# A rotation kernel: the buffers of the last eight outputs, taken in the other order

## Chip, cores, metric

The kernel runs on one core of one Trainium2 chip. The metric is device time in microseconds (us), lower is better. The runs were made on several chips, and the kernel before was timed again each time: its median was 1269.72, 1269.82, 1270.10 and 1269.99 us, and a single run of it 1269.89 us.

## The reference

```python
x = np.random.randn(8192, 8192).astype(np.float32)
np.rot90(x, 1)          # counter-clockwise: out[i, j] = x[j, 8191 - i]
```

It is a pure move: 268.44 MB are read and 268.44 MB written, and nothing is computed.

## The kernel before

The matrix is cut into 16 macro tiles of 1024 rows by 4096 columns, the last of them into two of 512 rows. A macro tile is loaded in pieces of 128 rows (2 MB each, issued on the SP queue). DVE copies each load, with the columns reversed in groups of 128, into eight small tiles `ar`, and after that the load buffer is free. PE transposes 128x128 blocks of `ar` into PSUM, ACT copies 2048 columns of PSUM at a time into an output buffer, and stores the output (2 MB, issued on the ACT queue). There are two load buffers (`a_pool`) and two output buffers (`o_pool`), 16 KB per partition each.

```python
    a_pool = ctx.enter_context(tc.tile_pool(name="a_pool", bufs=2))
    r_pool = ctx.enter_context(tc.tile_pool(name="r_pool", bufs=68))
    o_pool = ctx.enter_context(tc.tile_pool(name="o_pool", bufs=2))
    # ... cut ...
    def store(r0, rt, c0, chunks, end, first):
        # ... cut: rows = rt * P; PW and G, column blocks per PSUM tile and per output ...
        for i, g0 in enumerate(range(0, W // P, G)):
            if end and (i + first) % 2 == 0:
                ot = a_pool.tile([P, F], dt, tag="a")
            else:
                ot = o_pool.tile([P, F], dt, tag="o")
            # ... cut: S ...
            for h in range(0, G, PW):
                # ... cut: 16 transposes on PE into the PSUM tile ps ...
                nc.scalar.copy(o[:, G - PW - h : G - h, :], ps)
                done = h + PW
                if done % S == 0:
                    # ... cut: dst ...
                    nc.scalar.dma_start(out=dst, in_=o[:, G - done : G - done + S, :])

    *most, before_last, last = tiles
    for m in most:
        store(*m, load(*m), False, 0)

    c1 = load(*before_last)
    c2 = load(*last)
    store(*before_last, c1, True, 1)
    store(*last, c2, True, 1)
```

The two last macro tiles have four outputs each, here called O1 to O8. When they are made no further load is to come, so that the load buffers serve as output buffers too. With `first` 1 the order is o, a, o, a and again o, a, o, a. The output made just before O1, the last of the macro tile before, is called o8 below, and the one before that o7.

Of the kernel before, what the change touches and what calls it, by code (L numbers as in the profile page):

```python
# [2 lines left out]

# [5 lines left out]

P = 128  # L10




R = 1024
RT = R // P
LAST = [4, 4]
W = 4096
CH = 512
F = 4096  # L20
FP = 2048


def whole_reads(nc):






    for fn in nc.m.functions:
        for block in fn.blocks:
            for n, ins in enumerate(block.instructions):
                if not isinstance(ins, mybir.InstDMACopy):
                    continue
                src = ins.ins[0]
                ap = [list(d) for d in src.ap]
                if len(ap) == 3 and ap[2][0] == 1 and ap[1][0] == ap[2][1]:
                    ap = [ap[0], [1, 1], [1, ap[1][1] * ap[2][1]]]
                    block.instructions[n] = copy.replace(  # L40
                        ins,
                        ins=[copy.replace(src, ap=ap)],
                        ant_dge_precooked=False,
                    )


def macro_tiles(N, M):

    tiles = [(r0, RT, c0) for r0 in range(0, N, R) for c0 in range(0, M, W)]
    r0, _, c0 = tiles.pop()  # L50
    for n in LAST:
        tiles.append((r0, n, c0))
        r0 += n * P
    return tiles


@with_exitstack
def kernel(
    ctx: ExitStack,
    tc: tile.TileContext,  # L60
    x: bass.AP,
    k: bass.AP,
    out: bass.AP,
):
    nc = tc.nc
    assert k == 1, f"only k=1 supported, got {k}"
    nc.at_finalize(whole_reads)

    N, M = x.shape
    dt = x.dtype  # L70

    consts = ctx.enter_context(tc.tile_pool(name="consts", bufs=1))
    ident = consts.tile([P, P], dt)
    make_identity(nc, ident)
# [4 lines that stand above are left out]
    psum_pool = ctx.enter_context(  # L79
        tc.tile_pool(name="psum", bufs=2, space=bass.MemoryType.PSUM)  # L80
    )

    loads = 0

    def load(r0, rt, c0):





        nonlocal loads
        chunks = {}
        for t in range(rt):


            if loads < RT and loads % 4 >= 2:
                a = o_pool.tile([P, W], dt, tag="o")
            else:
                a = a_pool.tile([P, W], dt, tag="a")
            loads += 1  # L100
            nc.sync.dma_start(  # L101
                out=a[:], in_=x[r0 + t * P : r0 + (t + 1) * P, c0 : c0 + W]
            )
            for j in range(W // CH):
                ar = r_pool.tile([P, CH // P, P], dt, tag="ar")
                nc.vector.tensor_copy(  # L106
                    out=ar[:],
                    in_=a[:, j * CH : (j + 1) * CH].rearrange(
                        "r (b m) -> r b m", m=P
                    )[:, :, ::-1],  # L110
                )
                chunks[t, j] = ar
        return chunks

    def store(r0, rt, c0, chunks, end, first):





        rows = rt * P
        PW = 1
        while 2 * PW * rows <= FP:
            PW *= 2
        G = PW
        while 2 * G * rows <= F:
            G *= 2
        for i, g0 in enumerate(range(0, W // P, G)):
            if end and (i + first) % 2 == 0:
                ot = a_pool.tile([P, F], dt, tag="a")  # L130
            else:
                ot = o_pool.tile([P, F], dt, tag="o")
            o = ot[:, : G * rows].rearrange("m (g f) -> m g f", g=G)

            S = PW if end and r0 + rows == N and g0 + G == W // P else G
            for h in range(0, G, PW):
                pt = psum_pool.tile([P, FP], mybir.dt.float32, tag="ps")
                ps = pt[:, : PW * rows].rearrange("m (g f) -> m g f", g=PW)
                for w in range(PW):
                    g = g0 + h + w  # L140
                    for t in range(rt):
                        nc.tensor.transpose(  # L142
                            ps[:, PW - 1 - w, t * P : (t + 1) * P],
                            chunks[t, g * P // CH][:, g % (CH // P), :],
                            ident,
# [5 lines that stand above are left out]
                    top = M - c0 - (g0 + done) * P  # L151
                    dst = out[top : top + S * P, r0 : r0 + rows].rearrange(
                        "(g m) f -> m g f", g=S
                    )
                    nc.scalar.dma_start(  # L155
                        out=dst, in_=o[:, G - done : G - done + S, :]
                    )

    tiles = macro_tiles(N, M)
    *most, before_last, last = tiles  # L160
    for m in most:
        store(*m, load(*m), False, 0)

    c1 = load(*before_last)
    c2 = load(*last)
    store(*before_last, c1, True, 1)
    store(*last, c2, True, 1)


# [1 line left out]
_INS = ['x', 'k']  # L171
_OUTS = [((8192, 8192), 'float32')]

_NUMBERS = {'k': 1}


# [26 lines left out]
```

## Time and profile before

| what | value | where it is read |
|---|---|---|
| time | 1269.72 us (1269.53 to 1270.23, 4 runs) | timings |
| busy share of PE, ACT, DVE | 56%, 37%, 28% | the page |
| moved by DMA from 50 to 1200 us | 428 GB/s, share 1.01 | windows |
| DMA share 1213 to 1217, 1221 to 1225 us | 0.54, 0.29 | windows |

DMA bounds the kernel: a share of about 1 means that all 16 DMA engines are busy. The page of the kernel before: the share of the 16 DMA engines in 40 slices of the span in tenths, what they moved, and the shares of the chain that ended last.

```profile
DMA  9999999999999999999999999999999999999989
GB/s 399 418 430 429 430 429 429 430 428 430 428 429 429 429 428 429 429 430 429 428 430 429 429 427 425 424 429 429 429 429 423 417 426 427 428 429 429 429 361 374
DMA out_dram<-ot 73%; ACT ot L147 19%; DMA a<-in_x_dram 4%; PE pt L142 1%; DVE ar L106 0%; ACTq L155 0%; SPq L101 0%; ACTq L147 0%; DVEq L106 0%
```

After the first two slices and up to the last two it moves 417 to 430 GB/s; the Trainium skill ("DMA: Bandwidth & Descriptors", Specifications) states a fabric ceiling of 435 GB/s. So the question is what happens in the last 50 us. The windows of the kernel before show it: per row the stretch and its length, busy time and count of PE, PE weight loads, DVE, ACT and POOL, then the granted PE clock, the DMA share and GB/s.

```profile
50.00:1200.00 1150.00, 660.45 (x3754) 626.39 (x3753) 324.36 (x937) 426.27 (x234) 0.00 (x0) 0.73 1.01 428
1213.00:1217.00 4.00, 3.35 (x16) 3.36 (x17) 0.00 (x0) 2.36 (x2) 0.00 (x0) 0.59 0.54 225
1217.00:1221.00 4.00, 2.03 (x18) 1.78 (x16) 2.77 (x8) 1.20 (x1) 0.00 (x0) 0.98 1.02 430
1221.00:1225.00 4.00, 3.28 (x30) 3.24 (x31) 0.00 (x0) 3.25 (x3) 0.00 (x0) 1.00 0.29 123
1225.00:1258.00 33.00, 22.87 (x197) 20.98 (x194) 0.00 (x0) 24.63 (x14) 0.00 (x0) 0.95 1.01 419
...
1264.00:1266.00 2.00, 0.00 (x0) 0.00 (x0) 0.00 (x0) 0.00 (x0) 0.00 (x0) 0.50 0.40 164
```

Two dips lose 4 x 0.46 = 1.8 us and 4 x 0.71 = 2.8 us of DMA time. The timeline of ACT of the kernel before says what the second is: start, length, engine, line, what, count, and in brackets the idle time before it and what ended that. The lines are the evictions and stores of o8, O1 and O2.

```profile
1211.73 3.63 ACT L147 COPY ot<-pt 128x2048 f32<-128x2048 f32 x2 [6.22 <-DMA out_dram<-ot]
1215.39 0.55 ACTq L155 DMA_DIRECT2D out_dram<-ot  x1
1219.80 3.63 ACT L147 COPY ot<-pt 128x2048 f32<-128x2048 f32 x2 [4.44 <-DMA out_dram<-ot]
1223.47 0.55 ACTq L155 DMA_DIRECT2D out_dram<-ot  x1
1224.19 3.64 ACT L147 COPY ot<-pt 128x2048 f32<-128x2048 f32 x2 [0.75 <-PE pt L142]
1227.85 0.55 ACTq L155 DMA_DIRECT2D out_dram<-ot  x1
```

O1 waits 4.44 us for a store to land, the one of o7 whose buffer it takes; O2, in a load buffer, waits for PE only. The chain that ended last, of the kernel before, goes over the same wait (start, length, what):

```profile
1205.54 14.19 DMA out_dram<-ot
...
1219.80 0.06 ACT ot L147
...
1221.56 1.88 ACT ot L147
...
1223.47 0.55 ACTq L155
```

And the timeline of DVE of the kernel before shows when the two load buffers come free: the copies of the last load but one end at 1210.8, those of the last load at 1220.7.

```profile
1208.03 2.77 DVE L106 COPY ar<-a 128x512 f32<-128x512 f32 x8 [7.08 <-DMA a<-in_x_dram]
1217.89 2.77 DVE L106 COPY ar<-a 128x512 f32<-128x512 f32 x8 [7.09 <-DMA a<-in_x_dram]
```

### The profile page before, as it was taken

Reading aid. Unit: us, or ns where it says so; the run is one execution under the profiler, and the core shown is the slowest. Engines: PE = TensorE matmul, PEld = TensorE weight load, DVE = VectorE, ACT = ScalarE, POOL = GpSimd, SP = SyncE. Lnnn points to the kernel's source line nnn. Section 1 sums busy time; section 2 is a strip of 40 time slices with the busy share of each in tenths; the row PEclk is TensorE's granted clock in tenths of the full one; section 3 lists DMA queues with packets and bytes.
Section 4 is the critical chain, followed back from the end, with each engine's and each line's share of the span. In section 5 each row is a group of like instructions: output and inputs, shape, how many; then the busy total and the mean of one; then the engine's idle time right before and its main releaser. Section 6 shows DMA issues by size and latency. Waiting matters only on the chain.

```text
span 1267.9 us, 10385 instructions
## 1 busy us (share of the span) xinstructions
PE 708.5 (56%) x4096; PEld 668.7 (53%) x4096; DVE 355.1 (28%) x1024; ACT 467.6 (37%) x257; POOL 0.7 (0%) x6
## 2 busy tenths in 40 slices
PE   1456555655655556555556556565564655656674
PEld 0356455654655545554555545464564654645663
DVE  4422322232223322232223222232222322232210
ACT  0333344333433343333433334333433334333454
POOL 0000000000000000000000000000000000000000
PEclk9976767677677776776778767778777677677697
DMA  9999999999999999999999999999999999999989
GB/s 399 418 430 429 430 429 429 430 428 430 428 429 429 429 428 429 429 430 429 428 430 429 429 427 425 424 429 429 429 429 423 417 426 427 428 429 429 429 361 374
DMA packets 37057, 537.55 MB, mean 424 GB/s; under 512 B 4112, under 2 KB 4112, under 8 KB 4112
## 3 DMA queue, kind: packets, MB, share of 16 engines
q10 hardware_dynamic: 18576, 268.44, 49.9%
q1 hardware_dynamic: 18432, 268.44, 49.8%
q8 instruction: 32, 0.52, 0.2%
q14 instruction: 17, 0.14, 0.0%
HBM read 268.44 MB, written 268.44 MB: 423 GB/s over the span
## 4 chain that ended last, share of the span: by engine, by line
DMA 77%; ACT 19%; PE 1%; issue 1%; DVE 0%; ACTq 0%; SPq 0%; DVEq 0%
DMA out_dram<-ot 73%; ACT ot L147 19%; DMA a<-in_x_dram 4%; PE pt L142 1%; DVE ar L106 0%; ACTq L155 0%; SPq L101 0%; ACTq L147 0%; DVEq L106 0%
## 5 line engine op out<-in xcount | busy, mean ns | idle before, releaser
L142 PE MATMUL pt<-ident,ar 128*128 128x128 f32 x4096 | 708.5, 353 | 542.9 <-ACT ot L147 462.9
L142 PEld LDWEIGHTS pt<-ident,ar 128*128 128x128 f32 x4096 | 668.7, 189 | 582.4 <-ACT ot L147 493.5
L147 ACT COPY ot<-pt 128x2048 f32<-128x2048 f32 x256 | 466.3, 1869 | 745.1 <-DMA out_dram<-ot 732.6
L106 DVE COPY ar<-a 128x512 f32<-128x512 f32 x1024 | 355.1, 421 | 865.6 <-DMA a<-in_x_dram 781.4
L147 ACT ACT_TABLE_LOAD x1 | 1.3, 1283 | 41.0 <-DVE ar L106 41.0
masks.py:199 POOL TENSOR_SCALAR_AFFINE_SELECT ident<-ident 128x128 f32<-128x128 f32 x1 | 0.3, 294 | 0.1
masks.py:197 POOL MEMSET ident<- 128x128 f32 x1 | 0.2, 205 | 0.3 <-POOLq L184 0.3
L184 POOL MEMSET const-uint8-127<- 128x1 uint8 x1 | 0.1, 103 | 0.0
L184 POOL MEMSET const-bfloat16-1.0<- 128x1 bf16 x1 | 0.1, 102 | 0.0
L184 POOL MEMSET const-float32-0.0<- 128x1 f32 x1 | 0.1, 99 | 0.2 <-issue 0.2
L184 POOL MEMSET const-float32-1.0<- 128x1 f32 x1 | 0.1, 99 | 0.0
## 6 DMA issues: line engine op xcount, KB each, us to landing
a<-in_x_dram SPq DMA_DIRECT2D x128, 2048.0 KB, 16.8
out_dram<-ot ACTq DMA_DIRECT2D x127, 2048.0 KB, 15.8
out_dram<-ot ACTq DMA_DIRECT2D x2, 1024.0 KB, 12.9
```

The costliest lines, as they stand in the source:

```text
L106: nc.vector.tensor_copy(out=ar[:], in_=a[:, j * CH : (j + 1) * CH].rearrange("r (b m) -> r b m", m=P)[:, :, ::-1],)
L142: nc.tensor.transpose(ps[:, PW - 1 - w, t * P : (t + 1) * P], chunks[t, g * P // CH][:, g % (CH // P), :], ident,)
L147: nc.scalar.copy(o[:, G - PW - h : G - h, :], ps)
L184: nc = _bacc.Bacc("TRN2", target_bir_lowering=False, num_devices=1)
```

## The change

The intent: when O1 is due, the buffer of the last load but one has long been free, while the next output buffer is still being stored. So O1 takes the load buffer, and the order becomes a, o, a, o for both macro tiles. Everything else stays; the instructions of every engine and their order are the same, only waits differ.

```diff
-    def store(r0, rt, c0, chunks, end, first):
+    def store(r0, rt, c0, chunks, end):
...
-            if end and (i + first) % 2 == 0:
+            if end and i % 2 == 0:
                 ot = a_pool.tile([P, F], dt, tag="a")
...
-        store(*m, load(*m), False, 0)
+        store(*m, load(*m), False)
...
-    store(*before_last, c1, True, 1)
-    store(*last, c2, True, 1)
+    store(*before_last, c1, True)
+    store(*last, c2, True)
```

## The prediction

> **What bounds the kernel now.** The transfers. The page has the 16 DMA engines busy in every slice; the windows give 428 GB/s from 50 to 1200 us, against PE 57%, ACT 37%, DVE 28% busy there. The Trainium skill ("DMA: Bandwidth & Descriptors", Specifications) states a fabric ceiling of 435 GB/s; the trace agrees. No bytes change, so only stretches in which DMA is not full can be won. By the windows there are two near the end: 1213 to 1217 us (share 0.54, 1.8 us lost) and 1221 to 1225 us (share 0.29, 2.8 us lost). After 1225 it is full.
>
> **What the change moves.** Nothing but the buffers of the last eight outputs (call them O1 to O8): from o,a,o,a,... to a,o,a,o,.... Instructions and their order stay; only waits differ. Before, O1 takes an output buffer whose store, issued at 1205.54, lands at 1219.72; the eviction of O1 starts at 1219.80, its store is issued at 1223.47, and its packets start 1.2 us later (1224.7). After, O1 takes the buffer of the last load but one, whose last DVE copy ends near 1210.8. O1 then waits for PE alone.
>
> **Cost on the critical path.** PE transposes O1 from 1213.65; at the granted clock of 0.5 the first half is done at 1217.28, the second at 1219.03. So ACT should evict O1 from about 1217.4, and issue its store at about 1221.0 instead of 1223.47: 2.4 us earlier. Packets then start at about 1222.2. The output buffer that O2 now needs is free at 1219.72, and O2 is bound by PE and ACT: store at about 1225.2 instead of 1227.85. O3 takes the last load's buffer, copied by 1220.7; O4 the buffer that lands near 1224.7: neither waits. From there ACT needs 4.31 us an output and DMA about 4.95, so DMA stays full and the lead is kept. The first dip is not touched: there the previous tile's last output waits for its buffer.
>
> **How much arrives at the end.** Most engines finish the earlier store near 1221.6 and idle 3.1 us; they gain about 2.5. But completions of one store spread: the last two of 16 come at 1224.0 and 1224.7 against 1222.0. (The skill, same page, "Why a DMA increments its semaphore by 16 and not by 1", says that engines finish independently; the trace agrees.) Those two idle only about 1.8 and 1.1 us, and can gain no more. At the end two engines are again 2 us late (1267.0 against 1265.2), each having carried a 16 KB instruction fetch after 1225. If those are not the early stragglers, the end moves by about 2.5 us; if one is, by 1.1 to 1.8.
>
> **Prediction.** 1267.3 us, eight times in ten between 1266.0 and 1269.2; 0.2% faster. Faster by over 2%: 0.5%; within 2%: 99%; slower: 0.5%.
>
> **What would show it.** In the timeline O1's eviction starts near 1217.4, ended by PE, not by a store; the O1 store is issued near 1221; the window 1221 to 1225 has a DMA share near 0.8 instead of 0.29; 1213 to 1217 stays near 0.54; busy times and bytes are equal; later ACT groups start about 2.5 us earlier and still wait for PE only.
>
> **What would make it wrong.** A different granted clock at 1213 to 1219: full clock lets O1 go some 2 us earlier, for at most 0.6 us more. A straggling engine that gets a later fetch would halve the gain. A later eviction that waits for a store, from buffers now alternating the other way, would give some back. Runs of before spread over 0.7 us.

## The result, and the profile after

| | median us | range | runs |
|---|---|---|---|
| before | 1269.72 | 1269.53 to 1270.23 | 4 |
| after | 1267.90 | 1267.83 to 1268.47 | 4 |

The change gains 1.82 us, 0.14%. The ratio is 0.9986 with a 95% interval of 0.9969 to 1.0003. The interval just includes 1, but the ranges do not touch, and two repeats on other chips gave 1267.92 (beside 1269.82) and 1268.06 (beside 1269.99). One single run of the changed kernel was at 1269.43; all others, 13 of 14, were under every run of the kernel before.

The windows of the changed kernel, for the same stretches:

```profile
50.00:1200.00 1150.00, 650.96 (x3763) 617.12 (x3761) 324.16 (x937) 425.87 (x234) 0.00 (x0) 0.74 1.01 428
1213.00:1217.00 4.00, 3.28 (x17) 3.28 (x18) 0.00 (x0) 2.43 (x2) 0.00 (x0) 0.57 0.55 233
1217.00:1221.00 4.00, 3.78 (x34) 3.50 (x33) 2.78 (x8) 3.65 (x2) 0.00 (x0) 1.00 0.98 414
1221.00:1225.00 4.00, 3.42 (x32) 3.19 (x31) 0.00 (x0) 3.54 (x2) 0.00 (x0) 1.00 0.90 381
1225.00:1258.00 33.00, 20.79 (x180) 19.13 (x178) 0.00 (x0) 21.91 (x13) 0.00 (x0) 0.89 1.01 418
1258.00:1260.00 2.00, 0.00 (x0) 0.00 (x0) 0.00 (x0) 0.00 (x0) 0.00 (x0) 0.50 0.99 410
1260.00:1262.00 2.00, 0.00 (x0) 0.00 (x0) 0.00 (x0) 0.00 (x0) 0.00 (x0) 0.50 0.94 389
1262.00:1264.00 2.00, 0.00 (x0) 0.00 (x0) 0.00 (x0) 0.00 (x0) 0.00 (x0) 0.50 0.22 90
1264.00:1266.00 2.00, 0.00 (x0) 0.00 (x0) 0.00 (x0) 0.00 (x0) 0.00 (x0) 0.50 0.01 4
```

Steady state and first dip are as before, the second dip is nearly gone (0.90 instead of 0.29). But look at the end: from 1262 to 1264 only a fifth of the DMA engines' time is used, although the last store completes only at 1265.0. The timeline of ACT of the changed kernel, o8, O1 and O2 again:

```profile
1211.80 3.63 ACT L147 COPY ot<-pt 128x2048 f32<-128x2048 f32 x2 [6.21 <-DMA out_dram<-ot]
1215.46 0.55 ACTq L155 DMA_DIRECT2D out_dram<-ot  x1
1217.14 3.65 ACT L147 COPY ot<-pt 128x2048 f32<-128x2048 f32 x2 [1.71 <-PE pt L142]
1220.82 0.55 ACTq L155 DMA_DIRECT2D out_dram<-ot  x1
1221.46 3.63 ACT L147 COPY ot<-pt 128x2048 f32<-128x2048 f32 x2 [0.67 <-PE pt L142]
1225.13 0.55 ACTq L155 DMA_DIRECT2D out_dram<-ot  x1
```

O1 waits for PE, 1.71 us, and its store goes out 2.65 us earlier (1220.82 against 1223.47). The chain of the changed kernel in that stretch no longer holds a store's landing between o8 and O1:

```profile
1213.72 3.40 PE pt L142 x16
...
1217.14 3.66 ACT ot L147 x2
...
1220.82 0.55 ACTq L155
```

The last store goes out 2.7 us earlier too (1251.01 against 1253.72), and yet the span is only 1.9 us shorter (1266.0 against 1267.9). The loss is in how the 16 engines finish. Each store counts a completion from each of 16 DMA engines; these times stand in the trace's semaphore records. For three stores: the 8th of the 16, called the typical engine below, and the last three in order, in us.

```
store          before: 8th, 14th, 15th, 16th          after: 8th, 14th, 15th, 16th
o8             1221.99 1222.06 1224.00 1224.69        1222.03 1222.12 1223.79 1224.86
O1             1230.20 1230.24 1230.25 1230.81        1227.58 1228.18 1228.77 1229.92
O8, 2nd half   1265.21 1265.65 1266.96 1266.98        1262.40 1264.32 1264.45 1265.02
```

The typical engine ends 2.8 us earlier, the last one 1.96 us. Before, 15 of the 16 engines completed O1 together (1230.10 to 1230.25), the sixteenth at 1230.81: they had all been idle ahead of it. By the packet records of that trace most engines ended o8 at 1221.54 to 1221.69 and got the first packet of O1 at 1224.68 to 1224.82, so that they idled some 3.1 us; the last two ended o8 at 1223.61 and 1224.21, and idled only some 1.1 and 0.5 us. After, the engine that was last at o8, 2.8 us behind the 8th, is still last at the end, 2.6 us behind. From o8 to the end it took 1265.02 - 1224.86 = 40.16 us for eight outputs, which is the pace of the others (35.0 us for the seven outputs from O1 on, before, is 5.0 each). It did not idle: its last packet of o8 ended at 1224.360, its next began at 1224.357.

An account of the DMA time, from the packet records of the two traces, agrees. In the mean of the 16 engines, the kernel before idles 4.63 us from 1213 to 1225, the changed one 2.09 us, 2.54 us less. From 1225 to the end of the last packet the one before idles 1.30 us, the changed one 1.90 us, 0.60 us more. The difference, 1.94 us, is what the last packet moved (from 1266.58 to 1264.63).

Two more profiles of the changed kernel were taken, with its repeats on other chips. There PE ran at a granted clock of 0.50 from 1213 to 1217 (0.57 in the profile above), O1's store went out at 1221.59 and 1221.70, and the typical engine ended at 1263.13 and 1263.31, 0.7 to 0.9 us later than above; yet the last completion came at 1265.20 and 1265.24, only 0.2 us later. In both, the engine that is late at o8 and the two that fall behind later end within 0.2 us of each other, so that these traces do not say which of them is last.

### The profile page after: what moved, and what is told of

It is laid out like the page before. It is cut to its first block, busy times and chain, and to the rows that moved or that the text cites. A ratio compares the mean times of both kernels' runs of the same rounds, so it can differ in the third digit from the quotient of the medians.

```text
span 1266.0 us, 10386 instructions
## 1 busy us (share of the span) xinstructions
PE 700.4 (55%) x4096; PEld 660.8 (52%) x4096; DVE 354.9 (28%) x1024; ACT 467.3 (37%) x257; POOL 0.7 (0%) x6
## 4 chain that ended last, share of the span: by engine, by line
DMA 78%; ACT 19%; issue 1%; DVE 1%; ACTq 0%; PE 0%; DVEq 0%
DMA out_dram<-ot 74%; ACT ot L147 19%; DMA a<-in_x_dram 3%; DVE ar L106 1%; ACTq L155 0%; PE pt L142 0%; ACTq L147 0%; DVEq L106 0%
## 5 line engine op out<-in xcount | busy, mean ns | idle before, releaser
L142 PE MATMUL pt<-ident,ar 128*128 128x128 f32 x4096 | 700.4, 350 | 548.3 <-ACT ot L147 465.9
L142 PEld LDWEIGHTS pt<-ident,ar 128*128 128x128 f32 x4096 | 660.8, 187 | 587.7 <-ACT ot L147 496.4
```

The costliest lines, as they stand in the source:

```text
L142: nc.tensor.transpose(ps[:, PW - 1 - w, t * P : (t + 1) * P], chunks[t, g * P // CH][:, g % (CH // P), :], ident,)
```

## Experiments

The theory to test has two parts. (1) All of the gain comes from one wait, that of O1. (2) Its size is set at the end by one DMA engine that has been late since long before the tail and has no idle time to win. The rival of (1) is that the new alternation of all eight outputs matters; that of (2), that the end follows the issue of the stores, for all engines alike. Sizes are under 1%, so that the timed runs had five rounds.

### Two parts of the change, each alone

First half: `store(*before_last, c1, True, 0)` and `store(*last, c2, True, 1)` in the kernel before.

```diff
-    store(*before_last, c1, True, 1)
+    store(*before_last, c1, True, 0)
     store(*last, c2, True, 1)
```

> Only the last macro tile but one takes the new order (O1 to O4 in a,o,a,o; O5 to O8 stay o,a,o,a). Theory (all of the gain is that O1 no longer waits for a store to land): 1267.9 us like the full change; O5 then follows O4 in the same pool and waits for the store of O2, landing near 1235.0, so ACT slips by about 0.6 us there, which the DMA backlog hides. Rival (the alternation of all eight outputs matters): over half of the 1.8 us is lost, 1269 us or more.

Measured: 1268.18 us (1267.82 to 1268.51), with the change at 1267.92 and before at 1269.82 on the same chip. O1's store went out at 1221.09. O5's was issued at 1238.87, 0.5 us behind the rhythm, and O7's at 1249.19, another 1.7 us behind, each after a wait for a store. The DMA engines did not notice: these two stores took 11.3 and 10.9 us from issue to landing, so that work was queued. The gain is that of the whole change within 0.3 us.

Second half, on another chip:

```diff
     store(*before_last, c1, True, 1)
-    store(*last, c2, True, 1)
+    store(*last, c2, True, 0)
```

> Only the last macro tile takes the new order (O5 to O8 in a,o,a,o; O1 to O4 stay o,a,o,a). Theory (the gain is the wait of O1 alone): nothing gained, 1269.8 us like the kernel before, within 0.4. Rival (half of the gain comes from the last macro tile): about 1268.9 us.

Measured: 1269.75 us (1269.56 to 1270.21) beside 1270.10 for before, ratio 0.9999 (0.9985 to 1.0013). Nothing is gained. So part (1) holds, and of the eight changed buffers one pays.

The changed kernel was repeated beside the first half:

> The changed kernel once more, as the mate of the other runs of this chip. 1267.9 us, 1.8 us (0.14%) under the kernel before, in every round by over 1 us; otherwise the first measurement was chance.

Measured: 1267.92 us (1267.48 to 1269.43), ratio 0.9987 (0.9975 to 1.0000). The gain repeats in the median, but not "in every round by over 1 us", as expected: one run was at 1269.43. On a third chip (below) the ratio was 0.9982 (0.9969 to 0.9996).

### Not any load buffer, but the free one

Here the two load buffers are named `a0` and `a1`, and O1 takes the one of the last load.

```diff
-                a = a_pool.tile([P, W], dt, tag="a")
+                a = a_pool.tile([P, W], dt, tag=f"a{used % 2}")
+                used += 1
...
-                ot = a_pool.tile([P, F], dt, tag="a")
+                ot = a_pool.tile([P, F], dt, tag=f"a{(used - 1 + i // 2) % 2}")
```

> The change with O1 in the buffer of the last load instead of the last but one. Its DVE copies end near 1220.7, so O1 is evicted from about 1220.8 and its store goes out near 1224.4: 3.6 us later than in the change, 1.0 us later than before. By then every DMA engine is idle, the late one too (free at about 1223.6), so here each us of delay should count in full. Theory: 1.0 us over before, about 1270.8 us; the last completion of the O1 store near 1231.8. Rival (the delay of one store does not matter that much, the gain had come with the load buffers as such): 1268.5 us or less.

Measured: 1269.98 us (1269.90 to 1271.67), before 1270.10, ratio 1.0003 (0.9990 to 1.0015). That is neither the 1270.8 of the theory nor the rival's 1268.5. The timelines of this run show why: of ACT,

```profile
1219.89 3.63 ACT L149 COPY ot<-pt 128x2048 f32<-128x2048 f32 x2 [4.10 <-DVE ar L108]
1223.56 0.55 ACTq L157 DMA_DIRECT2D out_dram<-ot  x1
```

and of DVE,

```profile
1217.04 2.77 DVE L108 COPY ar<-a 128x512 f32<-128x512 f32 x8 [7.06 <-DMA a<-in_x_dram]
```

O1 now waits for the DVE copies of the last load, as meant. But in this run the last load landed some 0.85 us earlier than in the kernel before (its copies start at 1217.04, not 1217.89), so O1's store was issued at 1223.56, within 0.1 us of before, and the time equals that of before. The forecast of the extra microsecond was wrong about the load; the rule that the issue of O1's store decides is kept, and the idea that load buffers as such help is refuted.

### More of the idle taken away

If stores alone decided, closing the first dip as well would pay again. Here O1 is made before o8, since its buffer is free at 1210.8 and that of o8 only at 1211.8 (the edit is shortened, and the comments are added):

```diff
+    store(*m, cm, False, range(7))     # the macro tile before, all but o8
+    # ... loads of the last two macro tiles, but the copies of the last load ...
+    store(*before_last, c1, True, [0]) # O1
+    store(*m, cm, False, [7])          # o8
+    # ... copies of the last load, then O2 to O8 ...
```

> The change, and O1 is made before the previous tile's last output (call it o8), as its load buffer is free at 1210.8 and that of o8 only at 1211.8: the O1 store goes out near 1214.5, the o8 store near 1218.2, the O2 store near 1223.5 instead of 1225.1. So the DMA dips at 1213 to 1217 and 1221 to 1225 should nearly go (about 1.5 us of idle less for most engines). Theory (the end is set by the one DMA engine that was already some 2.8 us behind at 1224.9 and never idles from there on): no gain, 1267.9 us within 0.4. Rival (the end is set by when stores are issued, for all engines alike): 1266.2 us or less.

Measured: 1267.86 us (1267.64 to 1267.95), the change 1267.92 on the same chip: no gain. The windows of this run:

```profile
1213.00:1217.00 4.00, 4.00 (x25) 4.00 (x24) 0.00 (x0) 3.17 (x2) 0.00 (x0) 0.63 0.69 291
1217.00:1221.00 4.00, 3.79 (x33) 3.55 (x32) 2.77 (x8) 2.32 (x3) 0.00 (x0) 0.94 0.89 377
1221.00:1225.00 4.00, 3.42 (x32) 3.15 (x30) 0.00 (x0) 3.39 (x2) 0.00 (x0) 1.00 0.94 397
...
1260.00:1262.00 2.00, 0.00 (x0) 0.00 (x0) 0.00 (x0) 0.00 (x0) 0.00 (x0) 0.50 0.65 270
1262.00:1264.00 2.00, 0.00 (x0) 0.00 (x0) 0.00 (x0) 0.00 (x0) 0.00 (x0) 0.50 0.16 66
```

The dips closed less than meant (o8's store went out at 1220.1, not 1218.2, because its evictions waited 0.83 and 1.00 us for PE, whose granted clock was 0.63 in the first of these windows). Still the typical engine completed the last store at 1261.65, 0.75 us before the change's 1262.40, and the last engine at 1264.91 against 1265.02. What was won for most engines arrived as a longer wait for the last: the share in 1260 to 1262 is 0.65 instead of 0.94.

A stronger form: the same, and O1 and o8 stored in halves of 1 MB from the SP queue as soon as each half is evicted.

```diff
+            if which in ([0], [7]):
+                S = PW
...
-                    nc.scalar.dma_start(
+                    queue = nc.sync if which in ([0], [7]) else nc.scalar
+                    queue.dma_start(
```

> As the run that makes O1 ahead of the previous tile's last output (o8), and both of these are stored in two halves of 1 MB from the SP queue, each as soon as its half is evicted. In the earlier run the o8 store went out at 1220.1, not at 1218.2, as PE was at half clock, so most engines ended only 0.7 us before those of the change. Here the O1 halves should go out near 1212.8 and 1214.6, those of o8 near 1217.3 and 1220.1: most engines should end 1.5 to 2 us before those of the change (last store complete near 1260.6 instead of 1262.3). Theory (the one late engine sets the end): still 1267.9 us within 0.4, with the last completion near 1265.0, over 4 us after most. Rival (the end follows the stores of all engines): 1266.4 us or less.

Measured: 1267.87 us (1267.60 to 1267.99); the changed kernel, repeated on the same chip as its mate, 1268.06 us (1267.06 to 1268.31), before 1269.99. The expectation for the mate was:

> The changed kernel again, as the mate of the run with halves on this chip: 1267.9 us within 0.4.

The windows of the run with halves:

```profile
1213.00:1217.00 4.00, 3.81 (x35) 3.53 (x34) 0.00 (x0) 3.71 (x3) 0.00 (x0) 1.00 0.97 406
1217.00:1221.00 4.00, 2.66 (x25) 2.38 (x22) 2.77 (x8) 0.66 (x2) 0.00 (x0) 1.00 1.01 420
1221.00:1225.00 4.00, 2.10 (x16) 2.10 (x17) 0.00 (x0) 3.62 (x2) 0.00 (x0) 0.90 0.80 332
```

The first dip is gone (0.97), the halves left at 1212.0, 1213.7, 1215.9 and 1217.7. But O2's store then went out at 1224.65 and O3's at 1230.22, and typical engines idled there instead: they ended at 1262.12, where the change has 1262.40. So this run is no stronger test than the one before it. It does show where the idle went: O2 takes the buffer of o7 and O4 that of o8, which come back only when the last engine has done its part (1220.91 and 1231.56), however early the others are (O3 between them waited for PE). The last completion was at 1264.75. Three ways of ordering the stores thus end at 1264.75 to 1265.02 (1265.24 with the further profiles of the change).

### Which engine is last

Behind the last store, on the same queue, five small copies from the last output buffer to a spare tile, of 15, 8, 7, 14 and 4 rows. By the Trainium skill ("DMA: Bandwidth & Descriptors", Why a DMA increments its semaphore by 16 and not by 1) a DMA of n rows, for these n, runs on the n lowest-numbered engines. The traces bear out the number of engines (the copies count 15, 8, 7, 14 and 4 completions at the end), but not which engines they are. If each engine takes its queue in order, the completions of a copy tell which engines are late; the traces fit this, as the four late completions of the last store below recur 0.17 to 0.18 us later in the copy of 15 rows. In the changed kernel:

```diff
+        if end and r0 + rows == N:
+            for n in (15, 8, 7, 14, 4):
+                e = consts.tile([P, P], dt, tag=f"e{n}")
+                nc.scalar.dma_start(out=e[:n, :], in_=ot[:n, F - P :])
```

> The change, and behind the last store on the same queue five small copies within the chip of 15, 8, 7, 14 and 4 rows, which by the Trainium skill (DMA: Bandwidth & Descriptors, Why a DMA increments its semaphore by 16 and not by 1) run on the lowest 15, 8, 7, 14 and 4 engines. Their completions come when each of those engines has finished its part of the stores. If the late engine is number 15, no copy completes near the last completion of the last store (about 1265.0), and all increments of the copy of 15 rows are there by about 1264.6; if it is number 7, the copies of 15, 14 and 8 rows complete with it and that of 7 rows does not. The time says nothing (some us longer than the change).

The same five copies in the kernel before:

> The kernel before, with the same five small copies behind its last store. In the changed kernel with these copies four engines were late; of the two among the lowest 8 and 7, one was also among the lowest 4 (about 1.4 us late) and the last of all was not (2.3 us late): number 4, 5 or 6. Theory (before the change every engine went idle ahead of O1, which took the old lateness away, and the end is set by two engines that had an instruction fetch after it): two engines complete near 1267.0, one of them among the lowest 4, and the copies of 8 and of 7 rows have just that one late completion, so the engine that is last in the changed kernel is within 0.5 us of the others here. Rival (the same engine is last in both kernels): the copies of 8 and 7 rows have a late completion that the copy of 4 rows has not.

Measured, one run each (1268.34 and 1270.13 us, state unknown): the late completions out of the trace's semaphore records, in us.

```
                changed kernel                         kernel before
last store      most to 1262.60; 1263.79 1264.24       most to 1265.57; 1266.85 1266.98
                1264.43 1264.76
copy, 15 rows   1263.97 1264.41 1264.60 1264.94        1267.02 1267.15
copy, 14 rows   1264.52 1264.58 1264.76 1265.52        1267.19 1267.32
copy,  8 rows   1264.14 1265.13                        none (last 1265.95)
copy,  7 rows   1264.33 1265.32                        none (last 1266.14)
copy,  4 rows   1264.70                                none (last 1266.11)
```

In the changed kernel the last engine adds about 0.19 us per copy (1264.76, 1264.94, 1265.13, 1265.32) and is among the lowest 7 but not the lowest 4: number 4, 5 or 6 by the skill's rule. In the kernel before the two late engines are numbers from 8 to 13, and engines 4 to 6 are not late. The rival "the same engine is last in both" is refuted; my guess that one of the late ones before would be among the lowest 4 was wrong too. So the change swapped what ends the kernel: an engine that is nothing special before is last after, in this trace by 0.33 us; in the two further profiles of the change it shares the last place with others.

Why two engines were 2 us late before was not tested by an experiment. The trace shows two 16 KB instruction fetches on a DMA queue of their own, at 1230.3 and 1248.4, each of about 0.93 us, and engines that fall 1.9 us behind just after: one engine is 0.6 us late in O1 (1230.81) and 1.9 us from O2 on (1237.02 against 1235.15), a second one from O5 on (1252.02). The packet records, which do not name the engine, put the first of these fetches on the late one: its last packet of O1 takes 0.996 us where 0.61 is usual, its completion is written at 1230.299 to 1230.308, when all the others have written theirs, the fetch runs from 1230.305 to 1231.240, and a packet of 1.015 us follows at 1231.226. Together that is 1.7 us of the 1.9. The same three follow each other in the changed kernel, at 1226.657, 1227.677 and 1228.599.

### An attempt to relieve the late engine

If the late engine were number 15, one output in which it moves nothing would let it catch up.

```diff
+    def parts(end, r0, i):
+        # the third of the last eight outputs goes in rows 0-119 and twice four rows
+        if end and r0 + 4 * P < N and i == 2:
+            return [(0, 120), (120, 124), (124, 128)]
+        return [(0, P)]
...
-                    nc.scalar.dma_start(
-                        out=dst, in_=o[:, G - done : G - done + S, :]
-                    )
+                    for a, b in parts(end, r0, i):
+                        nc.scalar.dma_start(
+                            out=dst[a:b], in_=o[a:b, G - done : G - done + S, :]
+                        )
```

> The change, with the third of the last eight outputs stored as rows 0 to 119, 120 to 123 and 124 to 127. By the Trainium skill (DMA: Bandwidth & Descriptors, Why a DMA increments its semaphore by 16 and not by 1) 120 rows run on the lowest 15 engines and 4 rows on the lowest 4, so engine 15 moves nothing of this output: 4.9 us less for it, about 1.2 us more for engines 0 to 3. The same page (Latency and other measured facts) calls engines 7 and 15 usually slower. Theory (one late engine sets the end) with engine 15 as the late one: the last completion of every later store moves from 2.7 us behind most others to that of the second latest, and the time falls by 0.3 to 0.8 us to about 1267.3. If the late engine is another: unchanged, or up to 1.2 us longer. Rival (all engines alike): unchanged or longer.

Measured: 1273.58 us (1272.80 to 1276.27), 5.7 us over the change, ratio to before 1.0034 (1.0021 to 1.0046). Both theories missed this. Windows of this run, one ahead of the store of O3 and two within it:

```profile
1225.00:1229.00 4.00, 3.40 (x32) 3.17 (x31) 0.00 (x0) 3.42 (x2) 0.00 (x0) 1.00 0.98 401
...
1233.00:1237.00 4.00, 1.23 (x6) 1.23 (x7) 0.00 (x0) 3.15 (x2) 0.00 (x0) 0.70 0.94 242
1237.00:1241.00 4.00, 4.00 (x21) 4.00 (x20) 0.00 (x0) 2.00 (x2) 0.00 (x0) 0.50 0.95 217
```

The engines were as busy as ever (0.94, 0.95) but moved a little over half as much: two thirds of the packets that began from 1232.6 to 1236 took 1.2 to 1.5 us, where those of a 128-row store take 0.61. Why is not shown. So this store of 120 rows cost more than it freed, and the run says nothing on the theory. It was also aimed wrongly: the later run with the small copies shows engine 15 on time, and the row of that page of the Trainium skill gives, as its best guess, a cause on the GpSimd path for DMAs (SWDGE) that it says the other path does not have; this kernel issues its DMAs from SP and ACT.

No version was found that beats the change: the two that reorder O1 and o8 are equal to it within 0.2 us.

## Why the prediction was right, and where it was off

- **What bounds the kernel**: right. Transfers fill all but the tail, and the tail alone changed.
- **Which wait goes**: right. O1's eviction started at 1217.14 (predicted 1217.4), ended by PE; its store was issued at 1220.82 (1221.0), O2's at 1225.13 (1225.2). Later evictions wait for PE alone, and the last whole output before O8 is stored at 1246.70 instead of 1249.42. Taking the first half of the change alone gave the gain, the second half gave none.
- **The two dips**: right. The first stayed at 0.55; the second rose to 0.90 (predicted near 0.8), and to 0.81 and 0.73 in the two further profiles.
- **Time**: 1267.90 us against 1267.3, inside the range of 1266.0 to 1269.2. The gain was 1.8 us where 2.4 was forecast. The range was wide: it held any gain from 0.5 to 3.7 us, so that the hit alone says little.
- **The term that was mis-sized**: the idle time of the two engines that are late at o8, "Those two idle only about 1.8 and 1.1 us, and can gain no more". By the packet records of the kernel before they idled about 1.1 and 0.5 us. With its 1.1 the prediction could let the last of them end at 1265.2 - 1.1 = 1264.1, ahead of the two engines delayed by a fetch, at 1267.0 - 2.5 = 1264.5; hence "If those are not the early stragglers, the end moves by about 2.5 us". The condition held in the traces: the two that are late at the end before are numbers 8 to 13, the straggler that counts is 4, 5 or 6 (by one run each, and the skill's numbering). The delayed engines did move by 2.5 us (1266.98 to 1264.45). But with 0.5 the straggler ends at 1264.7, after them: that is what the prediction missed. Measured it ended at 1265.02; it was also 0.17 us later at o8 in that trace, and the rest is not accounted for. So the end moved by 1.96 us. The same follows from the spread at o8 alone: 2.7 us behind the typical engine before, carried to that engine's new end, 1265.2 - 2.8 = 1262.4, gives 1265.1.
- **How sure this is**: three things are shown. The engine that is last in the changed kernel is not one of the two that are last before (one trace of each with the small copies). It does not catch up with the typical engine in any trace of the changed kernel. And closing more idle for the others does not shorten the kernel (with O1 made before o8 the typical engine ended 0.75 us earlier, and the time was unchanged). What makes that engine late is open. In the trace of before the 16 completions of a load issued at 10.85 us lie within 0.4 us of each other, those of one issued at 580.38 us within 8.1 us, and those of one issued at 1200.98 us within 8.9 us: most of the spread arises in the first half. Instruction fetches are a candidate that the packet records offer. Right after one of 8 KB at 36.67 us a packet takes 1.265 us, and one of the 16 completions of the load then landing is 0.8 us behind the next, for the first time; another at 1212.88 us is followed at once by a packet of the last load that belongs to the engine that ends this load last. No run tests whether they make up the lag.

## What to carry to other kernels

At the end of a transfer-bound kernel, give an output the buffer that is free first at that moment, and read which one that is from the timeline; one output was worth all of the gain here, and the buffer of the last load, when tried, was worth nothing (1269.98 us against 1270.10). A filled gap in the average DMA share is worth only what it gives the engine that finishes last: look at the spread of a transfer's 16 completions before counting idle time as gain, read how long the last engine itself was idle (0.5 us here, where the typical one was idle for 3.1), and carry its lag to the end. When one dip closes and the time does not move, look for the same idle time later, as a longer tail or a new wait for a buffer.

## What the Trainium skill lacked or had wrong

- "DMA: Bandwidth & Descriptors", Latency and other measured facts, calls engines 7 and 15 usually slower in traces and offers a best guess that is specific to SWDGE. This kernel's DMAs are issued from SP and ACT, so it does not contradict the page; what is missing is which engines fall behind on these queues. Here, with the engines numbered by the same page's rule for few rows, the last engine was one of 4 to 6, and 7 and 15 were on time (7 by 1262.7 in the copy of 8 rows, where the last was at 1265.13; 15 by 1262.6 in the last store).
- The same page, Why a DMA increments its semaphore by 16 and not by 1, gives the rule for the engines that a DMA of 120 rows runs on, but no page says what it costs: 217 to 242 GB/s at a DMA share of 0.94 to 0.95, and 5.7 us more for one store of 2 MB split in that way.
- No page says that the engines drift apart in a long stream: the spread of a load's 16 completions grew from 0.4 us at 27 us to 8.1 us at 597 us and 8.9 us at 1218 us.
- No page says what an instruction fetch costs the data on its DMA engine: here 0.93 us for 16 KB, with a packet of about 1.0 us instead of 0.61 before it and another after it, about 1.7 us in all.
